# A planned transformer block: earlier gate Tanh, closer merge and turn, riders spread anew, split FFN norm, earlier tail splits

## The chip, the cores and the metric

The kernel runs on one core of a Trainium2 chip. The metric is the device time in microseconds of one execution of the whole program, lower is better. TensorE multiplies, VectorE (DVE in the profile) and ScalarE (ACT) do the elementwise work, SyncE (SP) issues the DMAs. GpSimd does nothing here.

## The reference

One layer of a diffusion backbone on 256 latent tokens and 256 context tokens of width 2048, all in float32. Cut to what matters:

```python
sh_m, sc_m, g_m, sh_f, sc_f, g_f = split(silu(c) @ w_ada + b_ada, 6)        # per sample
hl = rmsnorm(x) * (1 + sc_m) + sh_m                                          # tokens, 256 x 2048
p  = hl @ w_in                         # 13376 columns: SSD | z | pool | Fourier | 3 x 2048 gates
y_ssd  = rmsnorm(ssd(p) * silu(z)) @ w_ssd_out
y_pool = (pool2d(u) @ w_pool) * pool_scale
y_four = real(fft2(u)) @ w_fourier
merged = sigmoid(g0) * y_pool + sigmoid(g1) * y_four + sigmoid(g2) * y_ssd
x = x + g_m * (merged @ w_out)
h2 = rmsnorm(x) * (1 + sc_f) + sh_f
x = x + g_f * ((silu(h2 @ w_gate) * (h2 @ w_up)) @ w_down)                   # D_FF = 5632
out = rmsnorm(x) * final_norm_w
```

The context goes through the SSD part alone and gives the states from which the latent scan starts.

## The kernel before

**Products in three passes.** A float32 product is made of three matmuls in the format fp32r: each operand is split into a high part (a copy to fp32r) and a low part (what the copy lost), and high × high, high × low and low × high are summed in PSUM (`mm3`, lines 131 to 133). For weights, ScalarE writes the high part `whi` (`split`, L124, CAST) and VectorE the low part `wlo` (L125).

**Stages.** The weights come in stages of 256 rows × 512 columns, 512 KB each. `tokens` makes the stages of one product of all 256 tokens (two halves t = 0, 1 of 128): a stage is 12 matmuls, and a product with K = 2048 has 8 stages. Its two accumulators come from a pool `acc` of four, so a product takes the accumulators that the product but one before it has left. `stream` walks through the list of stages and writes the program in this order for stage i: loads up to stage i + lead + 3, splits up to stage i + lead, the matmuls of stage i, then some steps of side work, then what hangs on the stage's end (`after`). `lead` is 2 unless a stage says otherwise. There are five buffers for raw weights and three for split ones, so the cast of stage i + 3 waits for the last matmul of stage i. Stages with `held` put their parts into the larger pool `H`.

**Side work.** Everything that is not a product of a stage is a generator in the list `beside`: the SSD scan, the norms, gates, merges, turns. After each stage `side(room)` adds 1.45 to a credit (at most 3.0), and every generator may take one step while the credit is above 0.2; a step yields its price. After a step with a positive price the next generator has its turn, and a negative price lets the same one go on. All engines run what is written for them in order, so where a step is written decides behind what it stands.

**Gates and merges.** For each of four column blocks n, `phase_gate(i, n)` makes the product of the gate columns of branch i (0 pool, 1 Fourier, 2 SSD); the generator `sig` then takes the Tanh of both halves on ScalarE (sigmoid is (1 + tanh(x/2)) / 2). The branch's own product follows, and `merge` multiplies it by the gate and adds it to `merged[n]` on VectorE, one half per step. When branch 2 is merged, `to_feature` (the turn M0 to M3) transposes `merged[n]` on TensorE and splits it into `mh` (fth in the profile) and `ml` (ftl), the stationary operands of w_out. The last turn, M3, is needed by stage 7 of 8 of the first w_out product. `phase_z` does the same kind of gating for the SSD output and `silu` for the FFN gate.

**Riders.** The other modulation vectors (g_m, sc_f, sh_f, g_f) are not made on TensorE. A rider (`Ada`) loads 128 rows × 1024 columns of w_ada, 512 KB, together with a stage's weights, and VectorE adds them, scaled, to `adacc` (L461). `plan_ada` spreads a list of riders evenly over a range of stages. 32 riders make g_m, 64 make sc_f and sh_f, 32 make g_f. In the order of the program the stages are: x and C columns, from `s_u` on pool, z and Fourier columns (100 stages), from `s_f` four Fourier gates and products (48 stages), from `s_q` four SSD gates and products (64 stages), from `s_o` the four w_out products, from `s_g` the FFN.

**FFN norm.** At the end of w_out, `norm_ffn(t)` makes the row factor r and a diagonal matrix `dg` of it; `turn(n)` transposes and scales x1[n] by a matmul with `dg`, applies scale Af and shift Sf per part of 128 channels (L1183, four ACTIVATEs), and splits the result into `h2h` and `h2l`. It is done for n = 0 to 3 and for both halves, between the last stages of w_out and the first of the FFN gate, which use n = 0 and 1 first.

**Tail.** `last_rows` makes the last 512 rows of w_ffn_down for n = 0 to 3, two stages each, and ends each block with a scaled add (`dn`, `x`), a Square whose sum goes to the last norm (`junk`), and for n < 2 a product with the norm's weight (`xo`). `finish(t)` scales the rows and stores them.

Of the kernel before, what the change touches and what calls it, by code (L numbers as in the profile page):

```python
# [13 lines left out]
AF = mybir.ActivationFunctionType  # L14
ALU = mybir.AluOpType

P = 128
D = 2048
KT = D // P
# [11 lines left out]
Z_OFF = 3136  # L31
POOL_OFF = 5184
FOUR_OFF = 6208
GATE_OFF = 7232
N_IN = 13376
D_FF = 5632
CH = 512
# [45 lines left out]
def hybrid_block(ctx: ExitStack, tc, io):  # L83
# [23 lines left out]
    def H(shape, dt=F32, nme="h"):  # L107
        return hp.tile(shape, dt, tag="H", name=nm(nme))
# [18 lines left out]
    def rows(w, k0, nk, c0, n):  # L127
        return w[k0 * P : (k0 + nk) * P, c0 : c0 + n].rearrange("(k p) n -> p k n", p=P)
# [7 lines left out]
    stages = []  # L136
# [31 lines left out]
    def spawn(key, gen, front=False):  # L168
        beside.insert(0, (key, gen)) if front else beside.append((key, gen))
# [9 lines left out]
    def need(*keys):  # L179

        for key in keys:
            while key not in ended:
                credit[0] -= abs(step(next(e for e in beside if e[0] == key)))
# [32 lines left out]
    def add(src, n, mm, **kw):  # L216
        stages.append(Stage(src, n, mm, **kw))
        return stages[-1]
# [619 lines left out]
    def mm_pair(ps, op, p, parts, ts, first, last):  # L838
        hi, lo = parts
        for t in ts:  # L840
            for k in range(2):
                ah, al = op(2 * p + k, t)
                mm3(ps[t], ah, al, hi[:, k, :], lo[:, k, :], first and k == 0, last and k == 1)

    def tokens(w, k0, nk, c0, op, done, first=None):

        ps = []
        n = nk // 2
        for p in range(n):
            def mm(parts, p=p):  # L850
                if p == 0:
                    ps.extend((acc(), acc()))
                mm_pair(ps, op, p, parts, range(2), p == 0, p == n - 1)
            st = add(rows(w, k0 + 2 * p, 2, c0, CH), CH, mm, first=first if p == 0 else None)
        st.after.append(lambda: done(ps))

# [62 lines left out]
    zss = C([P, 8], nme="zss")  # L919

    def phase_z(g):
        def gated(ps):
            zz = H([P, 2, CH], nme="zz")
            ths = []
            for t in range(2):
                ths.append(Q([P, CH], nme="zt"))
                S.activation(ths[t], ps[t], AF.Tanh, scale=0.5)
            yield 0.0
            for t in range(2):
                V.scalar_tensor_tensor(zz[:, t, :], ths[t], 1.0, ps[t], ALU.add, ALU.mult)  # L930
            yield 1.2
            while f"s{g}" not in ended:
                yield 0.0
            for t in range(2):
                V.tensor_tensor(y[g][:, t, :], y[g][:, t, :], zz[:, t, :], ALU.mult)
            yield 1.2
            for t in range(2):
                junk = Q([P, CH], nme="junk")
                S.activation(junk, y[g][:, t, :], AF.Square, accum_out=zss[:, 2 * g + t : 2 * g + t + 1])
            yield 0.0  # L940

        tokens(w_in, 0, KT, Z_OFF + g * CH, h_op, lambda ps: spawn(f"z{g}", gated(ps), True))


    dh, dl = [None] * 2, [None] * 2
# [30 lines left out]
    def phase_gate(i, n):  # L976
        def sig(ps):
            gates[i, n] = []
            for t in range(2):
                g = Q([P, CH], nme="gt")  # L980
                S.activation(g, ps[t], AF.Tanh, scale=0.5)  # L981
                gates[i, n].append(g)
            yield 0.0

        tokens(w_in, 0, KT, GATE_OFF + i * D + n * CH, h_op, lambda ps: spawn(f"g{i}{n}", sig(ps), True))

    def merge(i, n, scale=None):
        def run(ps):
            need(f"g{i}{n}")
            gt = gates[i, n]  # L990
            new = merged[n] is None
            if new:
                merged[n] = H([P, 2, CH], nme="mg")
            for t in range(2):
                m = merged[n][:, t, :]
                o = m if new and scale is None else gt[t]
                V.scalar_tensor_tensor(o, gt[t], 1.0, ps[t], ALU.add, ALU.mult)
                if scale is not None:
                    V.tensor_tensor(m if new else o, o, scale[0], ALU.mult)
                if not new:  # L1000
                    V.tensor_tensor(m, m, gt[t], ALU.add)
                yield 1.2

        def done(ps):
            spawn(f"m{i}{n}", run(ps), True)

        return done
# [157 lines left out]
    def norm_ffn(t):  # L1165

        if t == 0:
            preload_sqrt(xss[:, 0, 0:1])
        r = rstd(xss[:, t, :], 1)
        dg = Q([P, P], nme="dg")  # L1170
        V.tensor_scalar(dg, ID, r, None, ALU.mult)
        if t == 0:
            for n in range(4):
                h2h[n], h2l[n] = H([P, 4, 256], F32R, nme="h2h"), H([P, 4, 256], F32R, nme="h2l")

        def turn(n):
            ps = aux([P, 4, P])
            hf = Q([P, 4, P], nme="h2")
            for c in range(4):
                T.matmul(ps[:, c, :], x1[n][:, t, c * P : (c + 1) * P], dg, start=True, stop=True)  # L1180
            for c in range(4):
                kt = 4 * n + c
                S.activation(hf[:, c, :], ps[:, c, :], AF.Identity, bias=Sf[:, kt : kt + 1], scale=Af[:, kt : kt + 1])  # L1183
            o = slice(t * P, (t + 1) * P)
            split(h2h[n][:, :, o], h2l[n][:, :, o], hf)

        return turn

    op_m, op_h2 = pair_op(mh, ml), pair_op(h2h, h2l)
    pg0 = []  # L1190
# [6 lines left out]
    def phase_o(n):  # L1197
# [80 lines left out]
        add(None, 0, mm_gate1, room=0)  # L1278
        for p in range(APART2, 8):
            st = add(rows(io["w_ffn_gate"], 2 * p, 2, 0, CH), CH, mm_gate(p))  # L1280
        st.after.append(lambda: spawn("a0", silu(0, pg0), True))


    ah, al = [None] * NFC, [None] * NFC
    sg = {}

    def silu(n, ps):
        sg[n] = []
        for t in range(2):
            s = Q([P, CH], nme="sg")  # L1290
            S.activation(s, ps[t], AF.Tanh, scale=0.5)
            sg[n].append(s)
        yield 0.0
        for t in range(2):
            V.scalar_tensor_tensor(sg[n][t], sg[n][t], 1.0, ps[t], ALU.add, ALU.mult)
            yield 0.6

    def glu(n, ps):
        need(f"a{n}")
# [20 lines left out]

    def phase_gate_up(n):
        if n > 0:
            tokens(io["w_ffn_gate"], 0, KT, n * CH, op_h2, lambda ps: spawn(f"a{n}", silu(n, ps), True))
        tokens(io["w_ffn_up"], 0, KT, n * CH, op_h2, lambda ps: spawn(f"b{n}", glu(n, ps), True))

    oss = C([P, 2, 5], nme="oss")
# [28 lines left out]
    def last_rows():  # L1355
# [61 lines left out]
        for n in range(4):  # L1417
            for p in range(2):
                add(rows(io["w_ffn_down"], 40 + 2 * p, 2, n * CH, CH), CH, mm_piece(n, p),
                    first=first if n + p == 0 else None, room=0.3 if n else 1.4, held=n > 1)  # L1420


    def all_ssd():
# [56 lines left out]
        phase_down(a, b)  # L1480
    last_rows()
    u_all = units_of(G_M, SC_F, SH_F)
    plan_ada(u_all[:32], s_u, s_q)
    plan_ada(u_all[32:], s_q, s_o + 10)
    plan_ada(units_of(G_F), s_g + 2, s_d - 4)
    load_upto(6)
    split_upto(1)
# [82 lines left out]
```

## Time and profile before

| | |
|---|---|
| median of 3 runs | 1902.11 us (1901.12 to 1902.36) |
| the profiled execution, its own time | 1902.28 us |
| its span, first to last instruction | 1900.5 us |
| granted TensorE clock, mean over the span | 0.992 |
| TensorE busy | 1845.0 us, 97% of the span |
| VectorE busy | 1247.2 us, 66% |
| ScalarE busy | 855.0 us, 45% |
| bytes read from HBM | 405.56 MB, 215 GB/s over the span |

A row of the page gives a line of the kernel, the engine, the operation, what it writes and reads (buffer numbers left out), the busy time and the mean of one in ns, and the engine's idle time just before it with what ended it. A row of a timeline gives start, duration, engine, line, operation, and in brackets the idle time before and its releaser.

### The profile page before, as it was taken

What the parts mean: (1) busy time and instruction counts of PE and PEld (TensorE: products, weight loads), DVE (VectorE), ACT (ScalarE), POOL (GpSimd) and SP (SyncE); (2) the same over time, 40 slices, a digit from 0 to 9 for tenths busy, and PEclk for the clock granted to TensorE, in tenths of its full rate; (3) what the DMA queues carried; (4) which work ended last, traced back from release to release, by engine and by line L of the source; (5) the groups of instructions that cost most, each with busy time, mean ns of one, the idle gap of its engine ahead of it and who ended that gap; (6) DMA issues with size and microseconds to landing.
All of it is one profiled execution on the core that took longest, in us unless ns stands there. A gap on an engine that the chain in (4) does not pass through costs nothing.

```text
span 1900.5 us, 23216 instructions
## 1 busy us (share of the span) xinstructions
PE 1845.0 (97%) x8796; PEld 1483.7 (78%) x8796; DVE 1247.2 (66%) x1508; ACT 855.0 (45%) x1216; POOL 0.2 (0%) x4
## 2 busy tenths in 40 slices
PE   5999999999999999999999998999999999999997
PEld 3667887777777788887777777888888888888885
DVE  4445785778777587777888654777655555555567
ACT  4323445637456474533434346444443444434434
POOL 0000000000000000000000000000000000000000
PEclk9999999999999999999999999999999999999998
DMA  9992332556657456789989754888756666556653
GB/s 330 358 342 75 114 112 67 179 169 216 201 163 242 142 178 211 220 256 321 332 315 322 267 199 129 284 282 288 257 190 196 190 188 188 190 197 189 191 192 127
DMA packets 211904, 409.19 MB, mean 215 GB/s; under 512 B 14672, under 2 KB 47568, under 8 KB 211792
## 3 DMA queue, kind: packets, MB, share of 16 engines
q1 hardware_dynamic: 211792, 407.71, 67.1%
q8 instruction: 69, 1.13, 0.3%
q14 instruction: 43, 0.35, 0.1%
HBM read 405.56 MB, written 2.10 MB: 215 GB/s over the span
## 4 chain that ended last, share of the span: by engine, by line
PE 81%; DMA 7%; DVE 5%; ACT 4%; issue 2%; SPq 1%; DVEq 0%; ACTq 0%
PE acc L131 23%; PE acc L133 23%; PE acc L132 23%; DMA raw<-w_ssd_out 4%; ACT whi L124 2%; PE aux L314 2%; DVE wlo L125 1%; DMA raw<-w_in 1%; DVE adacc L461 1%; DMA raw<-w_out 1%; PE aux L131 1%; PE aux L132 1%; PE aux L133 1%; PE aux L683 1%; PE aux L759 1%
## 5 line engine op out<-in xcount | busy, mean ns | idle before, releaser
L125 DVE TENSOR_TENSOR wlo<-raw,whi 128x1024 fp32r<-128x1024 f32 x548 | 669.4, 1223 | 564.9 <-ACT whi L124 559.9
L124 ACT CAST whi<-raw 128x1024 fp32r<-128x1024 f32 x548 | 575.3, 1052 | 805.0 <-PE acc L133 613.5
L131 PE MATMUL acc<-whi,h2h 128*128 128x512 f32 x700 | 273.6, 391 | 4.4 <-ACT h2h L124 4.4
L133 PE MATMUL acc<-whi,h2l 128*128 128x512 f32 x700 | 273.1, 390 | 0.0
L132 PE MATMUL acc<-wlo,h2h 128*128 128x512 f32 x700 | 272.6, 389 | 0.0
L131 PE MATMUL acc<-whi,lh 128*128 128x512 f32 x640 | 256.7, 401 | 3.5 <-ACT gt L981 3.3
L132 PE MATMUL acc<-wlo,lh 128*128 128x512 f32 x640 | 250.5, 391 | 2.4 <-DVE wlo L125 2.4
L133 PE MATMUL acc<-whi,ll 128*128 128x512 f32 x640 | 249.7, 390 | 0.0
L131 PEld LDWEIGHTS acc<-whi,h2h 128*128 128x128 f32 x700 | 131.5, 188 | 31.8 <-ACT h2h L124 5.0
L461 DVE SCALAR_TENSOR_TENSOR adacc<-araw,sil,adacc 128x1024 f32<-128x1024 f32 x120 | 153.4, 1278 | 2.1 <-DMA araw<-w_ada 2.0
L133 PEld LDWEIGHTS acc<-whi,h2l 128*128 128x128 f32 x700 | 131.5, 188 | 28.3 <-DVE h2l L125 0.9
L132 PEld LDWEIGHTS acc<-wlo,h2h 128*128 128x128 f32 x700 | 131.6, 188 | 27.1
L132 PEld LDWEIGHTS acc<-wlo,lh 128*128 128x128 f32 x640 | 120.3, 188 | 31.5 <-DVE wlo L125 5.6
L131 PEld LDWEIGHTS acc<-whi,lh 128*128 128x128 f32 x640 | 120.2, 188 | 31.5 <-ACT gt L981 4.1
L133 PEld LDWEIGHTS acc<-whi,ll 128*128 128x128 f32 x640 | 120.1, 188 | 25.3
L131 PE MATMUL acc<-whi,ah 128*128 128x512 f32 x336 | 131.0, 390 | 0.0
L133 PE MATMUL acc<-whi,al 128*128 128x512 f32 x336 | 130.7, 389 | 0.0
L132 PE MATMUL acc<-wlo,ah 128*128 128x512 f32 x336 | 130.7, 389 | 0.0
L131 PE MATMUL acc<-hh,whi 128*128 128x512 f32 x256 | 104.9, 410 | 3.6 <-ACT whi L124 3.6
L132 PE MATMUL acc<-hl,whi 128*128 128x512 f32 x256 | 100.5, 393 | 0.0
L133 PE MATMUL acc<-hh,wlo 128*128 128x512 f32 x256 | 100.5, 392 | 0.0
L133 PEld LDWEIGHTS acc<-whi,al 128*128 128x128 f32 x336 | 63.1, 188 | 13.1
(291 smaller groups left out, 2272.6 us busy)
## 6 DMA issues: line engine op xcount, KB each, us to landing
raw<-w_in SPq DMA_DIRECT2D x208, 512.0 KB, 4.2
araw<-w_ada SPq DMA_DIRECT2D x128, 512.0 KB, 4.9
raw<-w_ffn_gate SPq DMA_DIRECT2D x88, 512.0 KB, 3.8
raw<-w_ffn_up SPq DMA_DIRECT2D x88, 512.0 KB, 3.8
raw<-w_ffn_down SPq DMA_DIRECT2D x88, 512.0 KB, 3.6
raw<-w_ada SPq DMA_DIRECT2D x64, 512.0 KB, 9.2
raw<-w_ssd_out SPq DMA_DIRECT2D x32, 512.0 KB, 6.1
raw<-w_out SPq DMA_DIRECT2D x32, 512.0 KB, 4.6
```

What stands on the lines that cost most here:

```text
L124: S.copy(hi, src)
L125: V.tensor_tensor(lo, src, hi.bitcast(F32), ALU.subtract)
L131: T.matmul(out, ah, bh, start=first, stop=False)
L132: T.matmul(out, ah, bl, start=False, stop=False)
L133: T.matmul(out, al, bh, start=False, stop=last)
L314: T.matmul(aps[j][32 * k : 32 * k + 32, o], stat[:, 4 * p + k, :], raws[j, i][:, k, :], start=p == 0, stop=p == 3)
L461: V.scalar_tensor_tensor(a, self.raw, sil[:, kt : kt + 1], a, ALU.mult, ALU.add)
L683: T.matmul(ps, btk[:, 2 + t, :], xc[d][t], start=t == 0, stop=t == 1)
L759: T.matmul(seg, m, rh, start=n == 0, stop=n == 3)
```

## The change

- The Tanh of a gate (`sig`), of z (`early` in `phase_z`) and of the FFN gate (`tanh_gate`) is written directly behind the product's last matmuls, through a new argument `early` of `tokens`, and no longer as a step of side work.
- A merge yields -1.4 for 1.2, so that its two halves can be written at one place, and no longer asks for the gate's step. The turn behind it follows accordingly.
- The first 28 riders of g_m (of 32) and the other 68 are spread over other ranges of stages.
- In `norm_ffn`, scale and shift for n = 1 and 3 go to VectorE.
- In the tail, the stages of n = 1 have lead 3 and 4, so that all four splits of n = 2 and 3 are written before the sums of n = 1.
- A step of `silu` is priced 0.7 for 0.6.

```diff
-    def tokens(w, k0, nk, c0, op, done, first=None):
+    def tokens(w, k0, nk, c0, op, done, first=None, early=None):
...
                 mm_pair(ps, op, p, parts, range(2), p == 0, p == n - 1)
+                if early and p == n - 1:
+                    early(ps)
             st = add(rows(w, k0 + 2 * p, 2, c0, CH), CH, mm, first=first if p == 0 else None)
         st.after.append(lambda: done(ps))
...
     def phase_z(g):
-        def gated(ps):
-            zz = H([P, 2, CH], nme="zz")
-            ths = []
+        ths = []
+
+        def early(ps):
             for t in range(2):
                 ths.append(Q([P, CH], nme="zt"))
                 S.activation(ths[t], ps[t], AF.Tanh, scale=0.5)
-            yield 0.0
+
+        def gated(ps):
+            zz = H([P, 2, CH], nme="zz")
             for t in range(2):
                 V.scalar_tensor_tensor(zz[:, t, :], ths[t], 1.0, ps[t], ALU.add, ALU.mult)
...
                 gates[i, n].append(g)
-            yield 0.0
-
-        tokens(w_in, 0, KT, GATE_OFF + i * D + n * CH, h_op, lambda ps: spawn(f"g{i}{n}", sig(ps), True))
+
+        tokens(w_in, 0, KT, GATE_OFF + i * D + n * CH, h_op, lambda ps: None, early=sig)
 
     def merge(i, n, scale=None):
         def run(ps):
-            need(f"g{i}{n}")
...
-                yield 1.2
+                yield -1.4
...
             for c in range(4):
                 kt = 4 * n + c
-                S.activation(hf[:, c, :], ps[:, c, :], AF.Identity, bias=Sf[:, kt : kt + 1], scale=Af[:, kt : kt + 1])
+                if n % 2:
+                    V.tensor_scalar(hf[:, c, :], ps[:, c, :], Af[:, kt : kt + 1], Sf[:, kt : kt + 1], ALU.mult, ALU.add)
+                else:
+                    S.activation(hf[:, c, :], ps[:, c, :], AF.Identity, bias=Sf[:, kt : kt + 1], scale=Af[:, kt : kt + 1])
...
-        st.after.append(lambda: spawn("a0", silu(0, pg0), True))
+        st.after.append(lambda: (tanh_gate(0, pg0), spawn("a0", silu(0, pg0), True)))
...
-    def silu(n, ps):
+    def tanh_gate(n, ps):
         sg[n] = []
         for t in range(2):
             s = Q([P, CH], nme="sg")
             S.activation(s, ps[t], AF.Tanh, scale=0.5)
             sg[n].append(s)
-        yield 0.0
+
+    def silu(n, ps):
         for t in range(2):
             V.scalar_tensor_tensor(sg[n][t], sg[n][t], 1.0, ps[t], ALU.add, ALU.mult)
-            yield 0.6
+            yield 0.7
...
-            tokens(io["w_ffn_gate"], 0, KT, n * CH, op_h2, lambda ps: spawn(f"a{n}", silu(n, ps), True))
+            tokens(io["w_ffn_gate"], 0, KT, n * CH, op_h2, lambda ps: spawn(f"a{n}", silu(n, ps), True),
+                   early=lambda ps: tanh_gate(n, ps))
...
                     first=first if n + p == 0 else None, room=0.3 if n else 1.4, held=n > 1)
+                if n == 1:
+                    stages[-1].lead = 3 + p
...
-    plan_ada(u_all[:32], s_u, s_q)
-    plan_ada(u_all[32:], s_q, s_o + 10)
+    plan_ada(u_all[:28], s_u, s_f + 12)
+    plan_ada(u_all[28:], s_f + 12, s_o + 16)
```

How this moves instructions is shown at three places, all on VectorE. The number behind a name is the buffer's. The first is the end of the SSD product of n = 0, where `gt` is the gate times the product, `mg` the sum over branches, `adacc` a rider, and `ftl` the low part that the turn M0 writes. Before:

```order
L997 SCALAR_TENSOR_TENSOR gt_7187<-gt_7187,acc_7173 128x512
L1001 TENSOR_TENSOR mg_3418<-mg_3418,gt_7187 128x512
L125 TENSOR_TENSOR wlo_7372<-raw_7293,whi_7371 128x1024
L461 SCALAR_TENSOR_TENSOR adacc_7351<-araw_7295,sil_98,adacc_7351 128x1024
L997 SCALAR_TENSOR_TENSOR gt_7189<-gt_7189,acc_7174 128x512
L1001 TENSOR_TENSOR mg_3418<-mg_3418,gt_7189 128x512
L125 TENSOR_TENSOR wlo_7395<-raw_7314,whi_7394 128x1024
L461 SCALAR_TENSOR_TENSOR adacc_7351<-araw_7316,sil_98,adacc_7351 128x1024
L125 TENSOR_TENSOR wlo_7425<-raw_7343,whi_7424 128x1024
L461 SCALAR_TENSOR_TENSOR adacc_7351<-araw_7345,sil_98,adacc_7351 128x1024
L125 TENSOR_TENSOR wlo_7460<-raw_7369,whi_7459 128x1024
L1138 SCALAR_TENSOR_TENSOR ftl_7444<-aux_7445,fth_7443 128x512
```

The same place after:

```order
L125 TENSOR_TENSOR wlo_7409<-raw_7346,whi_7408 128x1024
L461 SCALAR_TENSOR_TENSOR adacc_6975<-araw_7348,sil_98,adacc_6975 128x1024
L999 SCALAR_TENSOR_TENSOR gt_7241<-gt_7241,acc_7254 128x512
L1003 TENSOR_TENSOR mg_3427<-mg_3427,gt_7241 128x512
L999 SCALAR_TENSOR_TENSOR gt_7243<-gt_7243,acc_7255 128x512
L1003 TENSOR_TENSOR mg_3427<-mg_3427,gt_7243 128x512
L125 TENSOR_TENSOR wlo_7436<-raw_7367,whi_7435 128x1024
L125 TENSOR_TENSOR wlo_7468<-raw_7386,whi_7467 128x1024
L461 SCALAR_TENSOR_TENSOR adacc_6975<-araw_7388,sil_98,adacc_6975 128x1024
L1140 SCALAR_TENSOR_TENSOR ftl_7452<-aux_7453,fth_7451 128x512
```

Both halves of the merge stand together, and between the merge's end and the turn's first split there are two weight splits and one rider for three and two.

The second place is the FFN norm, second half of the rows: `h2l` are the low parts of n = 0 to 3, `wlo_9329` that of the second of the stages whose matmuls come next. Before:

```order
L125 TENSOR_TENSOR h2l_9205<-h_9315,h2h_9204 128x4x128
L125 TENSOR_TENSOR wlo_9329<-raw_9178,whi_9328 128x1024
L125 TENSOR_TENSOR h2l_9207<-h_9333,h2h_9206 128x4x128
L125 TENSOR_TENSOR h2l_9209<-h_9351,h2h_9208 128x4x128
L125 TENSOR_TENSOR h2l_9211<-h_9369,h2h_9210 128x4x128
```

After:

```order
L125 TENSOR_TENSOR h2l_9205<-h_9315,h2h_9204 128x4x128
L125 TENSOR_TENSOR wlo_9329<-raw_9178,whi_9328 128x1024
L1186 TENSOR_SCALAR h_9333<-aux_9332,Af_382,Sf_383 128x128 x4
L125 TENSOR_TENSOR h2l_9207<-h_9333,h2h_9206 128x4x128
L125 TENSOR_TENSOR h2l_9209<-h_9351,h2h_9208 128x4x128
L1186 TENSOR_SCALAR h_9369<-aux_9368,Af_382,Sf_383 128x128 x4
L125 TENSOR_TENSOR h2l_9211<-h_9369,h2h_9210 128x4x128
```

The four operations of n = 1 stand behind `wlo_9329`, and those of n = 3 behind the low part of n = 2.

The third place is the tail; `hlo` are the low parts of the held stages, `dn`, `x` and `xo` the sums of a block. Before:

```order
L125 TENSOR_TENSOR hlo_14542<-raw_14458,hhi_14541 128x1024
L125 TENSOR_TENSOR hlo_14560<-raw_14476,hhi_14559 128x1024
L1377 TENSOR_TENSOR dn_14569<-acc_14545,g_10194 128x512
L1378 TENSOR_TENSOR x_8715<-x_8715,dn_14569 128x512
L1387 TENSOR_TENSOR xo_14574<-x_8715,t_14482 128x512
L1377 TENSOR_TENSOR dn_14582<-acc_14552,g_10194 128x512
L1378 TENSOR_TENSOR x_8715<-x_8715,dn_14582 128x512
L1387 TENSOR_TENSOR xo_14574<-x_8715,t_14482 128x512
L125 TENSOR_TENSOR hlo_14589<-raw_14503,hhi_14588 128x1024
L125 TENSOR_TENSOR hlo_14600<-raw_14539,hhi_14599 128x1024
L1377 TENSOR_TENSOR dn_14609<-acc_14592,g_10911 128x512
```

After:

```order
L125 TENSOR_TENSOR hlo_14542<-raw_14458,hhi_14541 128x1024
L125 TENSOR_TENSOR hlo_14546<-raw_14476,hhi_14545 128x1024
L125 TENSOR_TENSOR hlo_14564<-raw_14503,hhi_14563 128x1024
L125 TENSOR_TENSOR hlo_14568<-raw_14539,hhi_14567 128x1024
L1384 TENSOR_TENSOR dn_14577<-acc_14549,g_10195 128x512
L1385 TENSOR_TENSOR x_8703<-x_8703,dn_14577 128x512
L1394 TENSOR_TENSOR xo_14582<-x_8703,t_14482 128x512
L1384 TENSOR_TENSOR dn_14590<-acc_14556,g_10195 128x512
L1385 TENSOR_TENSOR x_8703<-x_8703,dn_14590 128x512
L1394 TENSOR_TENSOR xo_14582<-x_8703,t_14482 128x512
L1384 TENSOR_TENSOR dn_14609<-acc_14596,g_10912 128x512
```

The second pair of `hlo` moved ahead of the six operations of n = 1.

More of the change, by code (lines that the diff above doesn't have):

```diff
@@ L940, in gated @@
             yield 0.0
-        tokens(w_in, 0, KT, Z_OFF + g * CH, h_op, lambda ps: spawn(f"z{g}", gated(ps), True))
+        tokens(w_in, 0, KT, Z_OFF + g * CH, h_op, lambda ps: spawn(f"z{g}", gated(ps), True), early=early)
     dh, dl = [None] * 2, [None] * 2
```

## Prediction

> **What bounds the kernel now.** I read the page first, then who TensorE waits for over the whole span, then the windows in which those waits lie, and last the timelines around the four places that the change touches.
>
> ```profile
> PE 1845.0 (97%) x8796; PEld 1483.7 (78%) x8796; DVE 1247.2 (66%) x1508; ACT 855.0 (45%) x1216; POOL 0.2 (0%) x4
> ...
> L461 DVE SCALAR_TENSOR_TENSOR adacc<-araw,sil,adacc 128x1024 f32<-128x1024 f32 x120 | 153.4, 1278 | 2.1 <-DMA araw<-w_ada 2.0
> ```
> ```profile
> PE aux L285 <- DVE xt L278: 11.8, 1, 11.8
> PE acc L131 <- ACT h2h L124: 6.2, 3, 2.3
> PE acc L132 <- DVE wlo L125: 5.4, 10, 0.8
> PE acc L131 <- ACT hhi L124: 3.4, 1, 3.4
> PE acc L131 <- ACT gt L981: 3.3, 2, 1.6
> PE acc L131 <- ACT fth L1137: 2.1, 1, 2.1
> PE acc L133 <- DVE ftl L1138: 1.3, 1, 1.3
> PE aux L1132 <- DVE mg L1001: 1.1, 1, 1.1
> ```
>
> The second row is a rider (below), 1.28 us of VectorE. TensorE is busy for 97% of the span; no matmul is removed by this change, so only waits can go. The columns of the second view are total, count and longest wait. The start (xt) stays. The rest are short waits at a few places, and each costs more than its gap, because a matmul is shown longer than its turn:
>
> ```profile
> 402.67 0.40 PE L131 MATMUL acc<-whi,lh 128*128 128x512 f32 x1
> 402.91 0.39 PE L132 MATMUL acc<-wlo,lh 128*128 128x512 f32 x1
> ```
>
> Starts are 0.23 apart, durations 0.40: every wait hides a further 0.17. It also gives the length of a token stage: 12 matmuls, 2.72 us. Now the stretches (busy per engine, then clock, DMA share, GB/s):
>
> ```profile
> 760.00:800.00 40.00, 39.99 (x188) 33.02 (x188) 29.94 (x42) 22.80 (x33) 0.00 (x0) 1.00 0.69 214
> 866.00:946.00 80.00, 76.63 (x343) 60.67 (x342) 66.02 (x64) 31.53 (x36) 0.00 (x0) 1.00 0.93 325
> 946.00:1063.00 117.00, 110.11 (x495) 86.55 (x494) 97.11 (x98) 47.45 (x57) 0.00 (x0) 0.97 0.92 323
> 1056.40:1063.20 6.80, 5.46 (x12) 3.84 (x13) 6.12 (x8) 2.58 (x4) 0.00 (x0) 0.51 0.90 331
> 1200.00:1250.00 50.00, 50.00 (x230) 41.59 (x229) 37.47 (x36) 21.44 (x23) 0.00 (x0) 1.00 0.85 282
> ```
> ```profile
> ACT whi L124 <- DMA raw<-w_ssd_out: 44.7, 27, 3.8
> ACT whi L124 <- DMA raw<-w_in: 32.3, 17, 3.5
> ```
>
> From 866 to 1063 (the third gates, w_ssd_out, the start of w_out) TensorE idles 3.37 + 6.89 = 10.3 us. The second fence, waits inside 866 to 1063, names the cause: the casts stand waiting for weights, 77 us in 44 waits. The DMA is the limit there.
>
> **The change part by part.**
>
> *Riders.* A rider loads 512 KB, as much as a stage's weights. Now 64 riders lie on the 74 stages from phase_q to the tenth of phase_o: 1.865 loads per 2.72 us, 359 GB/s asked, 324 given. After, 68 lie on 116 stages: 1.586 loads, 306 GB/s at most. The FFN stretch has 1.5 loads per stage, moves 282 and has TensorE busy 50.00 of 50.00. So 306 lies between a rate that costs nothing and one that the queue has delivered; I take it as delivered. What it can win: the 10.3 us idle, 15 waits × 0.17 = 2.5, and the half clock after the long waits for fth and ftl (0.49 × 5.46 = 2.7, I take 2.5): 15.3 us. Two things remain. Merge and turn stand closer: for branch 2, n = 0 the transposes now follow one stage behind the merge. With T the end of the last product, VectorE does wlo (T+1.1 to 2.3), a rider of 1.28 and the merge of 2.7 (four operations like dn below), until T+6.2, and TensorE is there at T+5.44: a new wait of 0.85. The other n have no rider at that place, or two stages. And some wlo waits will stay: 1.5. Net **-12.9**; ends -15.3 and -4 (if two thirds of the waits only move). The last turn, M3, is emitted two stages earlier, so fth and ftl should not be waited for.
>
> The riders' first half hardly changes (32 on 148 stages, 28 on 112). But the Fourier stretch gets 0.59 riders per stage for 0.22: VectorE there is at 29.94 of 40.00, and 0.37 × 1.28 / 2.72 adds 17%, some 92% while the norm of y runs. In the new order that norm ends 11 stages later than now, 13 before it is needed. Short wlo waits are likely: **+0.7**, ends 0 and +4.
>
> *Tanh behind its product.* The wait for gt, twice:
>
> ```profile
> 404.94 1.05 ACT L124 CAST whi<-raw 128x1024 fp32r<-128x1024 f32 x1 [3.89 <-PE acc L133]
> 407.66 1.04 ACT L124 CAST whi<-raw 128x1024 fp32r<-128x1024 f32 x1 [1.66 <-PE acc L133]
> 408.61 1.08 ACT L981 ACTIVATE gt<-acc 128x512 f32<-128x512 f32 x2
> 409.25 0.50 PE L131 MATMUL acc<-whi,lh 128*128 128x512 f32 x1 [1.63 <-ACT gt L981]
> ```
>
> The product ended at 404.9; its Tanh stood behind two casts, the second of which waits for TensorE, and the next gate needs the accumulator. After, Tanh runs at 404.9 to 406.0 and the accumulator is free 1.6 us before it is asked for: 2 × (1.63 + 0.17) = **-3.6**. The 25 other products have no such wait and gain nothing. But ScalarE now waits for the product with all that stands behind: mostly the next cast, which waits for the same end anyway. That cast and wlo are done at T+2.3, needed at T+5.4, so 1.08 is covered by 3 us. At two ends (second pool gate, second z) an SSD step of operands stands between:
>
> ```profile
> 433.12 2.46 ACT L747 ACTIVATE rh<-cc,dah 128x128 fp32r<-128x128 f32 x8
> 435.47 1.27 ACT L752 ACTIVATE W<-cbf,ddt 128x128 f32<-128x128 f32 x4
> ```
>
> 1.08 + 3.7 + 1.05 + 1.23 gives wlo at T+7.1, needed at T+6.6 (the four matmuls of the step push TensorE by 0.9): 0.5 late, at z with an Exp ahead 1.0. **+1.2**, ends 0 and +4.
>
> *FFN norm, odd parts on VectorE.*
>
> ```profile
> 1142.20 0.29 DVE L1171 TENSOR_SCALAR dg<-cc,r 128x128 f32<-128x128 f32 x1
> 1143.39 0.62 ACT L124 CAST h2h<-h 128x512 fp32r<-128x512 f32 x1
> 1156.91 1.04 ACT L124 CAST whi<-raw 128x1024 fp32r<-128x1024 f32 x1 [5.79 <-PE acc L133]
> 1157.86 1.50 ACT L1183 ACTIVATE h<-aux,Sf,Af 128x128 f32<-128x128 f32 x4
> 1157.99 1.23 DVE L125 TENSOR_TENSOR wlo<-raw,whi 128x1024 fp32r<-128x1024 f32 x1 [6.14 <-ACT whi L124]
> 1160.07 0.50 PE L131 MATMUL acc<-whi,h2h 128*128 128x512 f32 x1 [2.30 <-ACT h2h L124]
> ```
>
> ScalarE takes 1.50 for four parts; VectorE at 0.29 each (the same shape, dg) 1.1. It helps only if VectorE is free, and it never is: part 1 of the first half comes behind dg, 1142.5 + 1.1 + 0.62 = 1144.2 against 1144.0 now. Part 3 stands behind h2l of part 2 (0.69 + 1.1 for 1.50). Part 1 of the second half stands behind wlo, which waits for the cast at 1156.91: 1159.2 + 1.1 + 0.62 = 1160.95 against 1160.0. Sum 0.2 + 0.3 + 0.9 = **+1.4**; ends -0.8 (the halves overlap after all) and +4.
>
> A rule against this part: the Trainium skill, "TensorE: Matmul & The Clock Gate", Part 1, says that TensorE drops to half clock after an idle window of about 3.4 us and needs as long a busy one to return. The trace agrees at one place, 0.51 after the 2.1 and 1.3 us of fth and ftl, though neither is 3.4 long alone. By it the third h2h wait, 2.3 now and 3.2 then, would tip over; see the rivals.
>
> *Tail splits.*
>
> ```profile
> 1871.19 1.98 ACT L124 CAST hhi<-raw 128x1024 fp32r<-128x1024 f32 x2
> 1872.42 2.35 DVE L125 TENSOR_TENSOR hlo<-raw,hhi 128x1024 fp32r<-128x1024 f32 x2
> 1874.69 0.68 DVE L1377 TENSOR_TENSOR dn<-acc,g 128x512 f32<-128x512 f32 x1
> 1878.19 0.69 DVE L1387 TENSOR_TENSOR xo<-x,t 128x512 f32<-128x512 f32 x1
> 1878.81 1.98 ACT L124 CAST hhi<-raw 128x1024 fp32r<-128x1024 f32 x2
> 1882.15 0.68 DVE L1377 TENSOR_TENSOR dn<-acc,g 128x512 f32<-128x512 f32 x1
> 1886.06 0.69 DVE L1377 TENSOR_TENSOR dn<-acc,g 128x512 f32<-128x512 f32 x1 [2.50 <-PE acc L133]
> 1887.51 0.63 ACT L1380 ACTIVATE junk<-x 128x512 f32<-128x512 f32 x1 [3.19 <-DVE x L1378]
> ```
>
> After, four casts and four hlo run in one piece: hlo until 1877.0, TensorE has its columns by 1879 and never waits the 3.4 us. Late next is VectorE: six operations of n = 1 (1874.69 to 1878.8 now, 4.1) until 1881.1, n = 2 until 1882.4, n = 3 until 1883.8. The last Square of the first half starts there for 1887.51: **-3.7**, not the 7 us that TensorE wins. Behind it everything is a chain on VectorE and ScalarE and moves along. Ends -4.2 and -2.5.
>
> Sum: -12.9 + 0.7 - 3.6 + 1.2 + 1.4 - 3.7 = -16.9. The profiled execution took 1902.28, 0.2 over the median of the runs, so 1885.4 on it and **1885** for the runs.
>
> **The rivals.**
>
> 1. *The DMA stays the limit, only longer.* For it: the share is already 0.85 at 282 GB/s. Against: 323 to 325 were moved. The 116 stages hold 184 loads, 96.5 MB. 116 × 2.72 are 316 us, and other matmuls come on top: of the 197 us from 866 to 1063, 15 are lost and 62 stages make 169, which leaves 13, 8%; so some 340 us, and 284 GB/s on average. At 270 GB/s the loads take 357, 17 us lost where I have 2.4: 1900. At 282 next to nothing. So 1889 to 1900.
> 2. *The turns wait instead.* Three turns lose distance to their merge; if casts come 3 us late as now, each costs up to 3: 1894.
> 3. *Slower: Tanh at the head of ScalarE's queue.* There are 27 such ends (12 gates, 4 z, 11 FFN gates). Price: whatever is issued between Tanh and the next cast no longer runs under the product. It decides from 17 / 27 = 0.63 us at each, that is with more than 2.6 us of other work behind each Tanh; then 1906 or more. Against: in the FFN ScalarE is busy 21.44 of 50.00.
> 4. *The half clock after the longer h2h wait.* 3.4 us at half speed lose 1.7: 1887.
> 5. *The spread changes nothing*, since the waits were the merges' and not the riders': loses the 12.9 but for M3's 6, 1892. Against: the 77 us of casts waiting for DMA.
>
> **How the numbers follow.** The forecast 0.62 (own range 1880 to 1890), the half clock 0.12, the DMA 0.09, turns or no effect of the spread 0.12, slower 0.05. Below 1877 only if every wait of 866 to 1063 and of the norm goes, above 1894 mainly the DMA and Tanh: range 1877 to 1894. A change of 0.2% (3.8 us) is about what a measurement tells from none: faster 0.91 (the four cases below 1898 but for a part of the DMA's), same 0.05 (that part, and a mild third rival), slower 0.04.
>
> **What would show it.** TensorE no longer waits for gt at the two pool products. Between 750 and 1080 the DMA is near 285 GB/s throughout, and casts wait for it for far less than 77 us. No fth or ftl wait. The three h2h waits sum to 7 to 8 us for 6.2. hhi is no longer waited for and the last Square of the first half moves by 3 to 4 us. It is wrong if casts still wait for weights there, or if whi is late behind many Tanhs.

## The result, and the profile after

| | before | after |
|---|---|---|
| median of the runs beside each other (5 each) | 1902.22 us (1901.12 to 1906.54) | 1891.59 us (1890.51 to 1896.62) |
| ratio to before, 95% interval | | 0.9946 (0.993 to 0.9962) |
| the profiled execution, and its span | 1902.28, 1900.5 | 1891.34, 1889.5 |

The change gains 10.6 us; 16.9 were forecast. The time lies inside the range, 6.6 above the forecast. First the waits of TensorE over the whole span of the changed kernel (total, count, longest, in us):

```profile
PE aux L285 <- DVE xt L278: 12.1, 1, 12.1
PE acc L131 <- ACT h2h L124: 8.3, 3, 3.4
...
PE aux L1105 <- DVE y L1095: 2.7, 2, 2.2
...
PE aux L718 <- DVE cbb L713: 1.6, 1, 1.6
...
PE acc L132 <- DVE wlo L125: 1.6, 3, 0.8
...
PE aux L705 <- DVE f L1073: 1.2, 1, 1.2
PE aux L1134 <- DVE mg L1003: 0.7, 1, 0.7
```

gt, fth, ftl and hhi are gone, and wlo has fallen from 5.4 to 1.6. New are y (the transposes of the normalized SSD output), cbb with 0.6 for another y (the scan), and f (the Fourier transform): waits that the prediction does not name. The windows of the changed kernel (busy per engine, clock, DMA share, GB/s), and the casts that wait for weights from 866 to 1063:

```profile
760.00:800.00 40.00, 40.00 (x186) 33.21 (x185) 32.50 (x38) 20.73 (x27) 0.00 (x0) 1.00 0.87 302
866.00:946.00 80.00, 79.31 (x366) 64.88 (x365) 60.08 (x60) 34.02 (x39) 0.00 (x0) 1.00 0.88 295
946.00:1063.00 117.00, 117.00 (x538) 96.44 (x537) 89.53 (x87) 48.87 (x56) 0.00 (x0) 1.00 0.86 298
```
```profile
ACT whi L124 <- DMA raw<-w_ssd_out: 8.0, 4, 2.4
ACT whi L124 <- DMA raw<-w_out: 2.1, 1, 2.1
```

Of 10.3 us idle there 0.7 are left. Of the 77 us in which casts waited for w_ssd_out and w_in 8 are left; with w_out, which the prediction's two rows leave out, it is 10 of 90.

Where the time went is best read by stage. The table gives the time between the first matmuls of certain stages in each profile: the kernel before, and the difference to it of the changed kernel and of six experiments below. The stretches are those of the program: up to `s_u`; pool; z and Fourier columns; Fourier gates; third gates; w_out; the end of w_out with the FFN norm; FFN; and the last 512 rows of w_ffn_down with the end.

| stretch | before | after | e1 riders + merge | e2 merge | e3 Tanh | e6 six buffers | e7 old first riders | e8 norm back |
|---|---|---|---|---|---|---|---|---|
| start | 349.2 | +0.8 | +2.0 | +2.8 | +1.9 | +0.7 | +1.3 | +1.3 |
| pool | 177.9 | -3.3 | +2.4 | -0.5 | -2.2 | 0.0 | -3.3 | -3.3 |
| z, Fourier columns | 173.9 | +2.1 | +2.1 | +4.1 | -0.2 | 0.0 | +2.6 | +3.8 |
| Fourier gates | 141.5 | +5.9 | +6.3 | +1.2 | +0.3 | 0.0 | +1.5 | +6.4 |
| third gates | 193.4 | -10.6 | -10.5 | -0.5 | +0.5 | -10.6 | -10.8 | -10.6 |
| w_out | 86.5 | -6.0 | -6.0 | -4.1 | +0.5 | -6.7 | -6.0 | -5.5 |
| norm | 53.1 | +3.7 | +1.6 | +1.2 | -0.1 | -1.1 | +2.9 | +1.5 |
| FFN | 686.4 | 0.0 | 0.0 | 0.0 | 0.0 | 0.0 | 0.0 | 0.0 |
| tail | 38.7 | -3.7 | +0.2 | +0.2 | +0.1 | +0.3 | -3.7 | -3.7 |
| span | 1900.5 | -11.0 | -2.0 | +4.5 | +1.0 | -17.4 | -15.5 | -10.1 |

The first row is not the change: apart from the buffers of e6, none of these kernels differs from before up to there, and the row moves by up to 2.8 us from run to run. A single profile's span is uncertain by that much. The rows below it repeat better: the FFN's agree within 0.03, and in e12, the changed kernel once more, all but two lie within 0.6 of the column "after". The two are the norm, +3.0 for +3.7, and z with the Fourier columns, +3.8 for +2.1, where half clock fell on the same waits (last section). A difference of up to 1.7 in one row of one profile is therefore not yet an effect of an edit.

### The profile page after: what moved, and what is told of

The parts are those of the page before. It is cut to its first block, busy times and chain, and to the rows that moved or that the text cites. A ratio compares the mean times of both kernels' runs of the same rounds, so it can differ in the third digit from the quotient of the medians.

```text
span 1889.5 us, 23230 instructions
## 1 busy us (share of the span) xinstructions
PE 1837.7 (97%) x8796; PEld 1482.7 (78%) x8796; DVE 1249.3 (66%) x1524; ACT 851.5 (45%) x1200; POOL 0.2 (0%) x4
## 4 chain that ended last, share of the span: by engine, by line
PE 90%; DVE 4%; ACT 3%; DMA 1%; issue 1%; SPq 1%; DVEq 0%; ACTq 0%
PE acc L131 26%; PE acc L132 26%; PE acc L133 26%; PE aux L314 2%; ACT whi L124 1%; PE aux L131 1%; DVE wlo L125 1%; PE aux L133 1%; PE aux L132 1%; PE aux L683 1%; PE aux L759 1%; SPq L105 1%; PE aux L1317 1%; PE aux L777 1%; DMA raw<-w_ada 0%
## 5 line engine op out<-in xcount | busy, mean ns | idle before, releaser
L133 PEld LDWEIGHTS acc<-whi,ll 128*128 128x128 f32 x640 | 120.1, 188 | 25.5
```

The costliest lines, as they stand in the source:

```text
L133: T.matmul(out, al, bh, start=False, stop=last)
```

## The experiments

A gain beside a ratio is worked out from the ratio.

**e1 and e2: which part brings the gain of the third gates.** e1 has the new ranges and the closer merge, which go together; e2 the merge alone.

```diff
-                yield 1.2
+                yield -1.4
```
```diff
-    plan_ada(u_all[:32], s_u, s_q)
-    plan_ada(u_all[32:], s_q, s_o + 10)
+    plan_ada(u_all[:28], s_u, s_f + 12)
+    plan_ada(u_all[28:], s_f + 12, s_o + 16)
```

> Before plus two parts of the change: the new rider ranges and the merge that yields -1.4 (the spread alone cannot be had, the two belong together); Tanh, norm and tail as before. My theory: the DMA was the limit from 866 to 1063, so most of the gain is here. The prediction's terms give -12.9 + 0.7 = -12.2 against before. The trace of the changed kernel suggests other sizes: about -16 from 850 to 1063, and +4.8 near 808 to 840, where TensorE waits for y behind wlo and a rider on VectorE: -11. There is a third place, +3.9 near 660 to 675 (TensorE waits for f, cbb and y of the scan). If that comes from the order that these two parts make, this run is -7; if it comes from the early Tanh of z, it is -11. Rival (the spread changes nothing, the merges were the wait): -6 or less, and the merge alone gives the same.

> Before plus the merge's yield of -1.4 alone, riders as before. Theory: the DMA stays the limit in the third gates, so waits for weights stay (10 us of idle TensorE from 866 to 1063), and only the last turn comes earlier: between -6 (fth and ftl no longer waited for, 3.4 idle and 2.5 of half clock) and +1 (the riders' lateness moves into other turns); I take -2. Rival: the merges were the wait, the riders not: the whole gain of the stretch, -12 or more, shows here.

e1: 1900.03 us, ratio 0.9973 (0.9964 to 0.9981), -5.1. e2: 1906.68 us, ratio 1.0007 (0.9998 to 1.0015), no change. The two together give the whole 10.5 of the third gates; the merge alone gives 0.5 there and 4.1 in w_out (the earlier M3). So the rival that the spread changes nothing falls. TensorE's waits in e1 from 640 to 860 show the new waits with the old Tanh:

```profile
PE aux L1103 <- DVE y L1093: 1.9, 2, 1.4
PE aux L718 <- DVE cbb L713: 1.6, 1, 1.6
PE acc L132 <- DVE wlo L125: 1.4, 2, 0.8
PE aux L705 <- DVE f L1071: 1.2, 1, 1.2
```

They come from riders and merge, not from Tanh. My -11 for that case is refuted, and my -7 was still 2 too good. In this profile the pool stretch is 2.4 longer: 0.8 because waits grew, gt's from 3.3 to 4.0, and 1.6 by half clock from 441.3 to 444.7, behind the second of them. e2 loses 4.1 in the z stretch although it moves no rider, with new short waits for wlo, btk, st and whi. As the planner is written, the merge's price changes the credit of the side work behind it; no run shows that by itself.

**e3: Tanh alone**, with the price 0.7.

```diff
+                if early and p == n - 1:
+                    early(ps)
...
-        tokens(w_in, 0, KT, GATE_OFF + i * D + n * CH, h_op, lambda ps: spawn(f"g{i}{n}", sig(ps), True))
+        tokens(w_in, 0, KT, GATE_OFF + i * D + n * CH, h_op, lambda ps: None, early=sig)
```

> Before plus the Tanh of gates, z and FFN gate behind the product alone (with silu's price 0.7), riders, merge, norm and tail as before. Theory: the two gt waits go, -3.6, and +1.2 for ScalarE's queue at three places: -2.4. If the waits near 660 to 675 in the changed kernel come from the early Tanh of z, +3.9 more: about 0. Rival 3 of the prediction (Tanh at the head of ScalarE's queue costs 0.63 us at each of 27 ends): +13.

1902.61 us, ratio 0.9984 (0.9976 to 0.9993), -3.0. The rival of 13 us is refuted: the FFN's 11 ends and the z stretch cost nothing. The pool stretch gains 2.2, not 3.6, since there is a new wait 13 us behind the second pool gate, in the fourth stage of the next pool columns:

```profile
448.27 0.50 PE L132 MATMUL acc<-wlo,lh 128*128 128x512 f32 x1 [1.33 <-DVE wlo L125]
```
```profile
444.28 1.99 ACT L124 CAST whi<-raw 128x1024 fp32r<-128x1024 f32 x2
```
```profile
443.41 0.68 DVE L999 SCALAR_TENSOR_TENSOR gt<-gt,acc 128x512 f32<-128x512 f32 x1
444.13 0.69 DVE L1001 TENSOR_TENSOR mg<-gt,psc 128x512 f32<-128x512 f32 x1
444.74 1.13 DVE L761 SCALAR_TENSOR_TENSOR W<-cbb,ddt,W 128x128 f32<-128x128 f32 x4
445.79 1.29 DVE L749 TENSOR_TENSOR rh<-dal,cc 128x512 fp32r<-128x512 f32 x2
446.99 2.35 DVE L125 TENSOR_TENSOR wlo<-raw,whi 128x1024 fp32r<-128x1024 f32 x2
```

The two casts are done by 446.3, the first of them about 445.3; wlo starts at 446.99, behind a merge and a step of the scan on VectorE. I had put 0.5 on ScalarE's queue nearer to that gate, at 441, where TensorE waits for nothing; here VectorE is what is late.

**e4: the tail alone.**

```diff
+                if n == 1:
+                    stages[-1].lead = 3 + p
```

> Before plus the earlier splits of the tail alone (lead 3 and 4). Theory: TensorE gains 7 us but VectorE's chain of n = 1 to 3 binds next: -3.7 (ends -4.2 and -2.5), hlo wait at the tail's start unchanged, hhi no longer waited for. Rival: the end is set by TensorE, and the whole 7 us come through; or by the norm's chain alone, and nothing does.

1899.70 us, ratio 0.9977 (0.9966 to 0.9989), -4.4; the tail's stretch is 3.7 shorter (38.66 to 34.99). The theory held; both rivals fall.

**e5: riders that load nothing.**

```diff
+                if unit.off != G_M:
+                    unit.raw = st.raw.rearrange("p k n -> p (k n)")
+                    continue
```

> Before, but the 64 riders of the second range and the 32 of the FFN load nothing: their VectorE operation reads the weights of the stage beside them (so sc_f, sh_f and g_f are not what the reference asks for). VectorE's work and its order are those of before, 512 KB less per rider are moved, and a rider takes no raw buffer. Theory (the weights come late from 866 to 1063): the casts no longer wait for weights and the 10.3 us of idle TensorE there go almost whole, with 2.5 hidden and 2 of half clock: -12 to -15. Rival (VectorE's 1.28 us per rider, or the distance from merge to turn, makes the waits): 0 to -6, and the turns and wlo waits stay.

1887.76 us, ratio 0.9915 (0.9897 to 0.9933), -16.2, a little more than the theory's 15. From 866 to 1040 no cast waits for weights any more, and TensorE is never idle, with VectorE's riders all there:

```profile
866.00:946.00 80.00, 80.00 (x376) 65.74 (x375) 69.76 (x70) 35.38 (x41) 0.00 (x0) 1.00 0.57 184
```

What bound the stretch were the loads, not VectorE and not the distance to the turn. But a rider that loads nothing takes no buffer either, so this run cannot tell rate from buffers.

**e6 and e10: six and four raw buffers.** Both are the kernel before.

```diff
-LEAD, RAWS, PARTS = 2, 5, 3
-HS, QS = 28, 17
+LEAD, RAWS, PARTS = 2, 6, 3
+HS, QS = 28, 15
```

> Before with six buffers for raw weights and riders for five (and two fewer of the small work tiles, to make room). Weights and riders share these buffers: at 1.865 loads per 2.72 us five of them are 7.3 us ahead, against 4.9 us from issue to landing and some 2.3 us until cast and subtraction have read them. Theory (the transfers' own rate is the limit, 324 GB/s moved at a share of 0.92): waits in 866 to 1063 hardly fewer, -2 (0 to -4). Rival (the five buffers are the limit, a load is issued too late): with six the stretch's 10.3 us go, -10 or better, and more than 330 GB/s are moved there.

> Before with four raw buffers for five. Theory (a load cannot be issued before a buffer is free, and that sets the rate): a round of the five buffers takes 5 x 0.524 MB / 324 GB/s = 8.1 us in the third gates; with four it gives 260 GB/s there, 3.8 us per stage where 2.72 are wanted and 3.0 are had, so 74 stages lose 55 more; the FFN's 1.5 loads per stage would also fall short, up to 19 more. +55 to +75, or as little as +25 if a transfer lands sooner with fewer beside it. Rival (the transfers' rate was the limit at 324): 324 GB/s stay and less than +10 is lost.

e6: 1885.59 us, ratio 0.9905 (0.9887 to 0.9922), -18.1. e10: 1938.66 us in one run, so without an interval, 34.5 above before on its chip. The windows of six buffers, then of four:

```profile
866.00:946.00 80.00, 80.00 (x377) 65.66 (x376) 71.12 (x71) 36.18 (x43) 0.00 (x0) 1.00 0.96 350
946.00:1040.00 94.00, 94.00 (x434) 76.60 (x433) 82.90 (x84) 38.59 (x45) 0.00 (x0) 1.00 0.96 346
```
```profile
866.00:946.00 80.00, 71.78 (x307) 53.56 (x307) 58.07 (x56) 28.81 (x34) 0.00 (x0) 1.00 0.84 285
946.00:1040.00 94.00, 83.39 (x362) 62.98 (x361) 69.32 (x70) 33.04 (x39) 0.00 (x0) 0.98 0.85 284
```

My theory of 324 GB/s as the transfers' own rate is refuted. With the riders' old, dense order 285, 325 and 350 GB/s move with four, five and six buffers, and TensorE stands idle for 8.2, 3.4 and 0 of the first 80 us. What six buffers could move at most stays open, since there TensorE asks for no more than 359. A load is issued when VectorE has released a buffer; what SyncE's queue waited for from 866 to 1063 in the kernel before said so:

```profile
SPq L105 <- DVE wlo L125: 96.7, 63, 4.0
SPq L105 <- DVE adacc L461: 38.2, 48, 1.4
```

135 of 197 us. The row alone does not decide (with six buffers it reads much the same, since the queue is then ahead), the size of the pool does. My price for four buffers (55 and more) took a round of buffers to last 8.1 us whatever their number; 4 x 0.524 MB at 285 GB/s is 7.4, so a round gets shorter with fewer in flight.

**e7: the first riders where they were.**

```diff
-    plan_ada(u_all[:28], s_u, s_f + 12)
-    plan_ada(u_all[28:], s_f + 12, s_o + 16)
+    for i, u in enumerate(u_all[:22]):
+        stages[s_u + i * (s_q - s_u) // 32].extra.append(Ada(*u))
+    plan_ada(u_all[22:], s_f, s_o + 16)
```

> The changed kernel with the riders of the first 100 stages (pool, z, Fourier columns) where before has them (22 of them), and the other 74 spread from s_f to s_o + 16. Theory: the waits for f, cbb and y of the scan near 660 to 675 come from the shifted order of side work in the first range, not from the Tanh; they go, -3.9 against the changed kernel (ratio near 0.9925 to before), while the waits for y in the Fourier stretch stay (0.58 riders per stage for 0.59) or move by up to 2. Rival: the scan's waits come from the closer merge or from Tanh of z, and nothing changes against the changed kernel (0.9946).

1887.04 us, ratio 0.9912 (0.9898 to 0.9927), -16.8 against before; both intervals of the changed kernel (0.993 to 0.9962 above, 0.9933 to 0.9958 in e12) lie outside. From 600 to 860 TensorE waits for f (1.2) and wlo (0.7); cbb and both y waits are gone. So the theory holds for cbb, and the wait for f has another cause. The y waits of the transposes went too, although 0.58 riders per stage stand where 0.59 did, so the number of riders does not make them. Nor does a rider directly ahead of y: VectorE has one there in e7 too (799.05, y at 800.25). Why y is in time in e7 was not found.

**e8: the norm on ScalarE again.**

```diff
-                if n % 2:
-                    V.tensor_scalar(hf[:, c, :], ps[:, c, :], Af[:, kt : kt + 1], Sf[:, kt : kt + 1], ALU.mult, ALU.add)
-                else:
-                    S.activation(hf[:, c, :], ps[:, c, :], AF.Identity, bias=Sf[:, kt : kt + 1], scale=Af[:, kt : kt + 1])
+                S.activation(hf[:, c, :], ps[:, c, :], AF.Identity, bias=Sf[:, kt : kt + 1], scale=Af[:, kt : kt + 1])
```

> The changed kernel with all four parts of the FFN norm on ScalarE again. From the trace of the changed kernel the norm's stretch is 3.7 longer than before: 2.2 from the diagonal matrix to the last h2h wait, 1.5 from half clock behind that wait of 3.4. Theory: -3.7 against the changed kernel (ratio near 0.9927), h2h waits back at 6.2 in all. The prediction's term said 1.4. Rival: the longer waits come from what the new riders left behind and not from VectorE's operations: no change.

1890.37 us, ratio 0.9926 (0.9911 to 0.9941), 3.8 us below the changed kernel's 0.9946, though the intervals overlap. In the profile the norm's stretch is 54.6, against 56.0 to 56.8 in four profiles with VectorE's operations (the changed kernel twice, e7, e11): 1.5 to 2.2 are shown as their doing. The half clock has little part in it, since all five profiles have three stretches of it here. The waits are short again, 6.4 for 8.3:

```profile
PE acc L131 <- ACT h2h L124: 6.4, 3, 2.3
```

**e11: y one step earlier than its transposes.**

```diff
             yield 0.8
+            yield 0.0
             pss = []
```

> The changed kernel with one more empty step between the scaling of y on VectorE and its transposes. Theory: TensorE waits near 808 and 823 because the scaling is written in the same place as the transposes' stage and stands behind wlo and a rider; a stage later it is done, and -3.1 goes (2.38 + 0.69 of lost time) against the changed kernel run beside it. Rival: VectorE is behind in the whole stretch, and the waits move to wlo or to yl: 0.

1888.37 us, ratio 0.9922 (0.9908 to 0.9936), 4.6 below the changed kernel beside it (0.9946). No wait of the transposes for y is left, and the Fourier gates' stretch is 144.7 for 147.4 and 148.0: 2.7 to 3.2, as expected. The rest of the 4.6 is no more than the intervals leave open.

**e12: the changed kernel again,** nothing edited.

> The changed kernel as it is, beside the three others on the same chip: ratio to before 0.9946 again (0.993 to 0.9962). If it came out elsewhere, the comparisons of e7 and e8 with it would have to be read with that shift.

1893.66 us, ratio 0.9946 (0.9933 to 0.9958), the same ratio again.

**e9: the best version:** the edits of e3, e4 and e6 on the kernel before.

> Before with six raw buffers, the early Tanh and the earlier tail splits; riders, merge and norm as before. The three parts alone gave ratios of 0.9905, 0.9984 and 0.9977, and in the trace of the six buffers the waits of the other two (gt 3.3, hhi 3.4) still stand. Theory: they add up, -18 - 3 - 4.4 = -25.5, near 1878. Rival: the parts overlap or the denser traffic brings the Tanh's casts late, -18 to -20.

1880.12 us, ratio 0.9875 (0.9861 to 0.9888): 23.8 below before and 13.5 below the changed kernel on the same chip. The parts' sum of 25.5 holds to 1.7. The three largest waits that TensorE has left, over the whole span:

```profile
PE aux L285 <- DVE xt L278: 12.3, 1, 12.3
PE acc L131 <- ACT h2h L124: 6.2, 3, 2.3
PE acc L131 <- ACT whi L124: 3.6, 1, 3.6
```

Third gates and w_out take 262.3 us here (279.9 before, 263.3 after), though the old rider order asks for 359 GB/s.

## Why the prediction was right in sign, and where its terms were off

| term, and the stretches that answer to it | predicted | measured |
|---|---|---|
| riders, turns: third gates and w_out | -12.9 | -16.6 |
| denser riders: z, Fourier columns and Fourier gates | +0.7 | +8.1 |
| Tanh and ScalarE's queue: pool | -2.4 | -3.3 |
| norm | +1.4 | +3.7 |
| tail | -3.7 | -3.7 |
| start, the same code | 0 | +0.8 |
| sum | -16.9 | -11.0 |

That the time lies inside the range is in part luck: two terms missed in opposite directions. Had the riders brought the -12.9 forecast for them and all else come as it did, the runs would stand at 1895.3, outside 1877 to 1894.

*Riders.* The term was too small, beyond its own end of -15.3, and its reason was half wrong. Idle time in the two stretches fell by 8.8 (10.26 to 1.47), where 8.0 was forecast (10.3 less 0.85 and 1.5). Of the rest, 0.65 is no gain: the nine matmuls that end a unit of riders now stand among the Fourier gates. What was mis-sized is the hidden part and the half clock, 7.1 for 5.0. The place and the cover were right: loads bound the stretch (e5), and with fewer loads per stage the waits go (e1). "I take it as delivered" held. What failed is "the DMA is the limit there": the limit was the five buffers (e6). Both cures end at the same floor, 182.6 to 182.9 us for the 64 stages in the changed kernel and in e1, e5, e6, e7, e8, e9, e11 and e12. The first rival, 270 to 284 GB/s as a lasting bound, falls with 350. The new wait at M0 came as worked out, 0.69 and a hidden 0.16 at 899 for 0.85.

*The Fourier stretch.* This is the step that failed: +0.7 for +8.1 (+10.3 in e12), beyond its end of +4. It charged VectorE's share of busy time, forecast as 92% and measured as 81% from 760 to 800 and 87% from 800 to 827, and looked for late wlo. Of the 8.1, 6.4 are new idle time of TensorE, 0.65 the nine matmuls that came over from the third gates, and the rest about what six waits hide at 0.17. The largest wait is for one operation in a wrong place, on VectorE and then on TensorE in the changed kernel:

```profile
806.20 1.28 DVE L461 SCALAR_TENSOR_TENSOR adacc<-araw,sil,adacc 128x1024 f32<-128x1024 f32 x1
807.40 0.88 DVE L1095 TENSOR_SCALAR y<-y,zss 128x512 f32<-128x512 f32 x2
```
```profile
808.02 1.29 PE L1105 MATMUL aux<-cc,y 128*128 128x128 f32 x8 [2.22 <-DVE y L1095]
```

The transposes are written one step of side work behind y. VectorE comes to y only behind wlo and a rider, and TensorE waits 2.2; with one step more between them the wait is gone (e11). The other part, 3.4 idle in the z stretch for f, cbb and the scan's y, goes against the sentence "The riders' first half hardly changes". By the planner's code a rider takes 1.2 from the credit of the side work, the end of a unit 1.3 and some steps more, and 28 riders on 112 stages put that end nine stages earlier than 32 on 148. The scan and the Fourier transform then meet otherwise on VectorE (f, cbb). e2 and e7 show that merge and riders each shift it. How much of the 8.1 each has is not settled: the parts do not add (e2 +5.3, e1 +8.4, e7 +4.1).

*Tanh.* The two gt waits went, as did the danger to the FFN. The +1.2 for ScalarE's queue did not show in the changed kernel (0.2 of wlo is its only wait in the pool stretch), and in e3 a wait of 1.3 on VectorE stands at another place: such a place depends on what else is written there.

*Norm.* Three things were left out or too small. On the changed kernel, VectorE, ScalarE, then TensorE:

```profile
1131.11 0.28 DVE L1173 TENSOR_SCALAR dg<-cc,r 128x128 f32<-128x128 f32 x1
1131.31 1.36 DVE L1186 TENSOR_SCALAR h<-aux,Af,Sf 128x128 f32<-128x128 f32 x4
```
```profile
1132.70 0.62 ACT L124 CAST h2h<-h 128x512 fp32r<-128x512 f32 x1 [1.83 <-DVE h L1186]
```
```profile
1151.20 0.50 PE L131 MATMUL acc<-whi,h2h 128*128 128x512 f32 x1 [3.43 <-ACT h2h L124]
...
1152.72 0.63 PE L132 MATMUL acc<-wlo,h2h 128*128 128x512 f32 x1
```

Four parts from PSUM take 1.36, not the 1.1 that I took from dg (which reads SBUF and has one operation for two; which of these counts was not tried), so each turn saves 0.14 on ScalarE's 1.50 and pays the queue. The three h2h waits sum to 8.3 (7 to 8 predicted). The fourth rival came about: behind the wait of 3.43 matmuls last 0.63 for 0.39. The waits account for 2.1 of the 3.7; the rest is that clock. The kernel before has two stretches of half clock in the norm, 3.41 us each; the changed kernel has three. So have e1, e2 and e8, where ScalarE does the norm, and e1's and e2's norms are 1.6 and 1.2 longer than before; the last section says on what the third depends.

*Tail.* Exact, and by the mechanism named. VectorE and ScalarE in the changed kernel:

```profile
1865.14 4.62 DVE L125 TENSOR_TENSOR hlo<-raw,hhi 128x1024 fp32r<-128x1024 f32 x4
1869.68 0.68 DVE L1384 TENSOR_TENSOR dn<-acc,g 128x512 f32<-128x512 f32 x1
```
```profile
1876.55 0.63 ACT L1387 ACTIVATE junk<-x 128x512 f32<-128x512 f32 x1 [0.60 <-DVE x L1385]
```

The chain of n = 1 starts behind the fourth hlo. From the tail's first hlo wait of TensorE (1866.41; 1873.69 before) to the last Square of the first half it is 10.1 us for 13.8: 3.7.

## What to carry to other kernels

When a stretch runs at 0.92 of the DMA's share and casts wait for weights, vary the number of buffers before calling the transfer rate the limit: one buffer more was worth 18 us here; the re-spreading of loads cured the same stretch, lost most of it again elsewhere, and was worth 5. Where a planner shares one credit among all side work, moving one kind of work shifts every later meeting of the others, so the waits to price are the operations that TensorE needs at once, not the busy share of the engine. An operation moved to a neighbour engine gains only if that engine has nothing queued ahead, and its price is best taken from a row of the same operation on the same source.

## What the runs showed of the hardware

A single core reading 512 KB pieces moved 285, 325 and 350 GB/s with four, five and six of them allotted. The Trainium skill, "Perfetto Trace Analysis", section "Engine Utilization", gives 358 GB/s as a core's share and more where one core is alone; the fastest of a page's 40 slices in any run here, near the program's start, is 359. Little of the more shows: in e6 368 over the 47 us from 1006 and 361 over the 80 us from 861, where one transfer is 11 and 7 GB/s of that.

The half clock does not hang on the length of a wait alone. The clock column of the windows, in the kernel before behind its third h2h wait (2.30), and in the changed kernel behind its own (3.43):

```profile
1160.00:1163.30 3.30, 3.23 (x13) 2.35 (x14) 1.39 (x2) 3.27 (x10) 0.00 (x0) 1.00 0.61 164
```
```profile
1151.20:1154.60 3.40, 3.40 (x9) 2.42 (x10) 2.04 (x5) 1.96 (x5) 0.00 (x0) 0.65 0.33 124
```

Behind 3.43 the slow matmuls came in all four profiles that have this wait and lost 1.7 to 1.9 us; the prediction's price was 1.7. Behind 2.30, the same wait in ten other profiles, they lost 1.6 to 1.8 in five (e1, e2, e5, e8, e10) and 0.2 in five.

What parts them is when the wait falls. In the clock record of every profile here, from 350 to 1860 us, half clock comes in blocks of 3.41 us, or two in one piece, and all blocks of one profile start whole multiples of 3.41 us apart, as on a grid. Counted in windows of that grid over the 14 profiles, TensorE was idle for 1.9 us or more of a window 31 times, and each time the next window ran at half clock. From 1.6 to 1.85 idle it went either way; with less it never did, unless the window itself was at half clock. The grid cuts the wait of 2.30: its larger part is 1.6 to 2.2 us in the five profiles with slow matmuls and 1.2 to 1.6 in the others. The changed kernel shows it on equal waits of the scan, 1.61 for cbb and 0.64 for y. In its first profile they lie in two windows, in e12 in one with 2.1 idle, and e12's z stretch is 1.6 longer. The clock, first profile and e12:

```profile
674.00:680.00 6.00, 5.37 (x21) 3.68 (x20) 5.78 (x9) 0.90 (x1) 0.00 (x0) 1.00 0.62 173
```
```profile
674.00:680.00 6.00, 5.11 (x11) 2.86 (x12) 6.00 (x10) 0.00 (x0) 0.00 (x0) 0.72 0.50 146
```

What sets the grid's place in a run is not shown; the kernels do nothing to set it. The Trainium skill, "TensorE: Matmul & The Clock Gate", Part 1, has the half rate follow an idle window of about 3.4 us. The blocks of 3.41 agree with that length. No window in that range was idle throughout, though (at most 3.24 of 3.41), and 1.9 was always enough. That differs from a wholly idle window, and the measurement decides.
